# All projections of a two-layer decoder trunk with tokens stationary, results and residual stream turned in 32x32 blocks through DRAM

## The chip, the core and the metric

The kernel runs on one core of a Trainium2 chip. A core has a matrix engine (TensorE, PE in the profile; its weight loads are PEld), a vector engine (VectorE, DVE), a scalar engine (ScalarE, ACT), GpSimd (POOL) and SyncE (SP), each with its own in-order queue of instructions. DMA transfers are issued from SP's and ACT's queues here and carried out by 16 DMA engines. Working memory is SBUF (128 partitions); TensorE writes into PSUM, in banks of 128 x 512 float32. The metric is the time of one execution on the device in microseconds (us): the median of several runs.

## What is computed

256 tokens of width 2048 go through two layers. The first mixes tokens with gated linear attention (GLA, 4 heads, in chunks of 64 tokens), the second with forgetting attention (FoX, 12 heads, causal softmax with a decay). Each layer also attends with 4 heads to 256 memory tokens, and each has a gated MLP with a causal convolution of width 3. Cut to its steps:

```python
mem_n = rmsnorm(mem, norm_mem)
# layer 0
mk, mv = memory_kv(mem_n, mem_w_kv[0])
h = rmsnorm(x, norm_mix[0])
q, k, v, glr, og, mq = split_cols(h @ gla_w_in, ...)
o = rms(gla_chunked(q, k, v, g(glr))) * gn_gain * silu(og)
x = x + concat([o, memory_attention(mq, mk, mv)]) @ gla_w_out
x = x + conv_ffn(rmsnorm(x, norm_ffn[0]), ...)
# layer 1
k, v, fl = split_cols(rmsnorm(x, fox_kv_norm) @ fox_w_kv, ...)
q, mq = split_cols(rmsnorm(x, norm_mix[1]) @ fox_w_in, ...)
x = x + concat([fox_attention(q, k, v, cumsum(log_f)), memory_attention(mq, ...)]) @ fox_w_out
x = x + conv_ffn(rmsnorm(x, norm_ffn[1]), ...)
return rmsnorm(x, norm_final)

def conv_ffn(h, w_up, conv_w, conv_b, w_down):
    a, val = split_cols(causal_dwconv(h @ w_up, conv_w, conv_b), ...)
    return (jax.nn.silu(a) * val) @ w_down
```

All is float32. Weights are read once: some 430 MB.

## The kernel before, in words

**Precision.** Every large product is made of three: an operand is split into a high part that TensorE takes as it is (type fp32r) and a low part, the rest. The product is high x high + high x low + low x high. Activations stand in 16 tiles `A0..A15` (`bufA`) or `B0..B15` (`bufB`), one for each 128 features, with high and low halves of 256 tokens each (`split`, lines 332 to 340).

**Units and panels.** Weights come in units of 512 KB (1024 columns in each of 128 partitions). For each unit SP issues one load into `raw` (line 215), ACT makes the high part `whi` (line 218) and DVE the low part `wlo` (line 227), with four buffers for `raw` and three each for `whi` and `wlo`. These three are issued with a higher priority than what stands around them. A panel is a set of units that fills one set of accumulators; `_panels` lists them in the order in which they run.

**Two forms of a panel.** `proj_fm` (line 231, feature-major) has 256 outputs: a unit holds four chunks of 128 inputs, the weights are TensorE's stationary operand, and the high and low tokens side by side (512 columns) stream past `whi` (line 246), the high tokens alone (256 columns) past `wlo` (line 254). Its result lies with features in partitions; the two halves of the accumulator are added by an ACT copy and a DVE addition (`whole`, lines 263 and 265). It serves the keys of both attentions and of the memory, all queries and the output gate `og`: 34 panels of 4 units. `proj_tm` (line 282, token-major) has up to 512 outputs: a unit holds two chunks of inputs, the tokens are stationary, and the weights stream (lines 276, 277 and 280, 512 columns each, for both blocks of 128 tokens). Its result lies with tokens in partitions. It serves values, output projections and both MLP matrices.

**Turning in the MLP.** The MLP needs features in partitions for its convolution. `panel` (line 870) scales the result on ACT (line 876), transposes its 32x32 blocks on DVE (line 877), writes the 512 KB to DRAM (line 880) and reads it back in four transfers (line 885), which puts the blocks in their places. `later` (line 185) sets when this happens: so many units after the panel, counted by `passed` at each unit, and each step is queued behind that unit's cast on ACT:

```python
later((3, write), (6, read), (8, lambda: taken(j, base, u, 0)), (9, lambda: taken(j, base, u, 1)))
```

**The residual stream** `x` lies with tokens in partitions, four tiles of 512 features. After an output projection (`add_out`) has added a block to x, `preparing` (line 898) turns it on TensorE in 128x128 transposes (line 915), and `split` (line 340) makes the next stage's activations of it with the norm's gain; the norm's scale itself is applied to results (`nx.col` in token-major panels; `nx.row`, a broadcast made on TensorE at line 396, in feature-major ones; `nx.mixed` in the MLP).

**Ends of stages.** `proj_two` (line 300) runs two panels together: the first units of both, then the last `late` units of both, so that chunks that become ready late are asked for late. It is used for the MLP's second matrix with `late` 1. The output projections (`wo`) run one panel after the other and begin with the memory heads' chunks.

**Order around the change.** Memory keys and values of both layers; GLA: `gv` of head 0, memory queries, then for each head `gq`, `gk`, `gv` and the chunked core (`core`, line 600, fed by `gates`, line 580), two `og` panels before the last head's values and four after; `wo`; MLP; `fk`, `fv`, memory queries, `fq` with `attend` (line 785) at once for each head; `wo`; MLP; final norm.

Of the kernel before, what the change touches and what calls it, by code (L numbers as in the profile page):

```python
# [19 lines left out]
P = 128  # L20
# [22 lines left out]
OG_EARLY = 2  # L43
# [13 lines left out]
def _panels():  # L57
# [16 lines left out]

    for l in range(2):
        for j in range(2):
            fm(("mk", l, j), ("mem_w_kv", l), j * 256)
        tm(("mv", l), ("mem_w_kv", l), 512, 512)
    tm(("gv", 0), ("gla_w_in", 0), G_V, DV, more=[(G_R, RANK)])
    for j in range(2):  # L80
        fm(("mq", 0, j), ("gla_w_in", 0), G_MQ + j * 256)
    for h in range(GLA_H):
        fm(("gq", h), ("gla_w_in", 0), G_Q + h * DK)
        fm(("gk", h), ("gla_w_in", 0), G_K + h * DK)
        for j in range(OG_EARLY if h == GLA_H - 1 else 0):
            fm(("og", j), ("gla_w_in", 0), G_OG + j * 256)
        if h:
            tm(("gv", h), ("gla_w_in", 0), G_V + h * DV, DV)
    for j in range(OG_EARLY, 6):
        fm(("og", j), ("gla_w_in", 0), G_OG + j * 256)  # L90
    late = list(range(12, 16)) + list(range(12))

    def ffn(l):
        for p, (lo, hi) in enumerate(PARTS):
            for j in range(lo, hi, 2):
                turned(("up", l, j), ("ffn_w_up", l), [c + k * P for c in (0, HID) for k in (j, j + 1)])
            for f in range(4):
                tm(("down", l, p, f), ("ffn_w_down", l), f * 512, 512, list(range(lo, hi)))

    for f in range(4):  # L100
        tm(("wo", 0, f), ("gla_w_out", 0), f * 512, 512, late)
    ffn(0)
    for j in range(6):
        fm(("fk", j), ("fox_w_kv", None), F_K + j * 256)
# [3 lines left out]
    for j in range(2):  # L108
        fm(("mq", 1, j), ("fox_w_in", 0), FOX_H * HD + j * 256)
    for j in range(6):  # L110
        fm(("fq", j), ("fox_w_in", 0), j * 256)
    for f in range(4):
        tm(("wo", 1, f), ("fox_w_out", 0), f * 512, 512, late)
# [26 lines left out]
M_ID, M_ONE, M_FOX, M_SCAN, M_LVL = 0, 128, 256, 512, 768  # L140
M_PICK = M_LVL + NVER * len(LEVELS)
M_N = M_PICK + 2 * T
# [3 lines left out]
def _trunk(ctx: ExitStack, tc: tile.TileContext, xt, xtok, memt, wp, wgu, gns, gfin, cnv, par, msk, out):  # L146
# [6 lines left out]
    sm = ctx.enter_context(tc.tile_pool(name="small", bufs=2))  # L153
    pacc = ctx.enter_context(tc.tile_pool(name="pacc", bufs=4, space=PSUM))
# [7 lines left out]
    foxmask = mask[:, M_FOX : M_FOX + T]  # L162
# [41 lines left out]
    def load_unit(unit, pieces=1, before=None, pool=wpool, whole=False):  # L204
# [5 lines left out]
        for i in range(pieces):  # L210
            if before is not None:
                before(i)
            s = slice(i * w // pieces, (i + 1) * w // pieces)
            if not whole:
                loads.append(nc.sync.dma_start(raw[:, s], src[:, s]))
            elif i == 0:
                loads.append(nc.sync.dma_start(raw[:, :w], src))
            casts.append(S.activation(hi[:, s], raw[:, s], AF.Copy))  # L218
        return raw, hi, w

    def split_unit(unit, pieces=1, before=None, pool=wpool, whole=False):
        with tc.high_priority(offset=AHEAD):
            raw, hi, w = load_unit(unit, pieces, before, pool, whole)
# [6 lines left out]

    def proj_fm(key, src, evac, before=None):

        units = where[key]
        acc = [pacc.tile([P, 512], F32, name="acc", tag="acc") for _ in range(2)]
        base = min(min(u[1]) for u in units)
        for n, unit in enumerate(units):
            if before is None:
                hi, lo = split_unit(unit)
            else:
                hi, lo = split_unit(unit, 2, lambda half: before(n, half), whole=n > 0)  # L240
            todo = [(j, kc, c) for j, kc in enumerate(unit[1]) for c in range(2)]
            end = n == len(units) - 1

            def high(j, kc, c, stop=False):
                s = slice(j * 256 + c * P, j * 256 + (c + 1) * P)
                TE.matmul(acc[c], hi[:, s], src[kc - base], start=n == 0 and j == 0, stop=stop)  # L246

            kept = todo[-2:] if end else []
            for t in todo:
                if t not in kept:  # L250
                    high(*t)
            for j, kc, c in todo:
                s = slice(j * 256 + c * P, j * 256 + (c + 1) * P)
                TE.matmul(acc[c][:, :T], lo[:, s], src[kc - base][:, 0, :], start=False, stop=False)  # L254
            for t in kept:
                high(*t, stop=True)
        for c in range(2):
            evac(c, acc[c])

    def whole(a):  # L260

        t = sm.tile([P, T], F32, name="part1", tag="part1")
        S.activation(t, a[:, T:], AF.Copy)
        r = sm.tile([P, T], F32, name="wholes", tag="wholes")
        V.tensor_tensor(r, a[:, :T], t, ALU.add)
        return r
# [15 lines left out]
    def proj_tm(key, src, evac, spare=None):  # L282
# [7 lines left out]
        for i in range(len(units) + ahead):  # L290
            if i < len(units):
                ready[i] = split_unit(units[i], pool=wpool if spare is None or i < 3 else spare)
# [39 lines left out]
    def split(dst, i, src, g=None):  # L332

        hi, lo = dst[i][:, 0, :], dst[i][:, 1, :]
        if g is None:
# [6 lines left out]
    class Norm:  # L342


        def __init__(self, n, tag="x"):
            self.n, self.tag = n, tag
            self.acc = self.y = self.r = self.m = None

        def add(self, src):
            sq = sm.tile([P, T], F32, name="sq", tag="sq", bufs=2)  # L350
            S.activation(sq, src, AF.Square)
            if self.acc is None:
                self.acc = sq
            else:
                acc = sm.tile([P, T], F32, name="ssq", tag="ssq", bufs=2)
                V.tensor_tensor(acc, self.acc, sq, ALU.add)
                self.acc = acc
# [30 lines left out]
        def row(self):  # L388

            if self.r is None:  # L390
                y = self.col()
                dg = sm.tile([P, T], F32, name="dg", tag="sq", bufs=2)
                for b in range(2):
# [4 lines left out]
                                 bufs=2 if self.tag == "x" else 1)  # L398
# [42 lines left out]
    def mem_attention(pool, l, q, hd, dst):  # L441
# [11 lines left out]
        pts = pool.tile([P, 512], F32, name="pts", tag="ed", bufs=2)  # L453
# [14 lines left out]
    with tc.tile_pool(name="load", bufs=1) as lp:  # L468
# [3 lines left out]
        def take_mem(g, half):  # L472

            if g == 0:
# [4 lines left out]
                chunks = range(2 * half, 2 * half + 2)  # L479
            else:  # L480
                if half == 0:
                    nc.sync.dma_start(mraw[g][:, KC:], memt[g, :, KC:])
                    if g == 1:
                        nc.sync.dma_start(gains, gns)
                chunks = range(2 * half, 2 * half + 2)
            for i in chunks:
# [3 lines left out]
        def mk_out(l, j):  # L490
            def evac(c, a):
                o = mk[l][:, 2 * j + c, :]
                if l == 0:
                    S.activation(o, a[:, T:], AF.Copy)
                    V.tensor_tensor(o, o, a[:, :T], ALU.add)
                    if c == 1 and j == 1:
                        for f in range(MEM_H):
                            V.tensor_tensor(mk[0][:, f, :], mk[0][:, f, :], nrm.row(), ALU.mult)
                else:
                    V.tensor_tensor(o, whole(a), nrm.row(), ALU.mult)  # L500

            return evac
# [4 lines left out]
        def first_out(c, a):  # L507
            mk_out(0, 0)(c, a)
            if c == 1:
                nc.sync.dma_start(mask[:, :M_FOX], msk[:, :M_FOX])  # L510
                sq, acc = [lp.tile([P, 4, T], F32, name=n) for n in ("sq4", "ssq4")]
                with tc.issue_after(casts[-1].ins):
                    for g in range(4):
                        S.activation(sq if g else acc, mt[g], AF.Square)
                        if g:
                            V.tensor_tensor(acc, acc, sq, ALU.add)
                V.tensor_tensor(acc[:, :2, :], acc[:, :2, :], acc[:, 2:, :], ALU.add)
                V.tensor_tensor(acc[:, 0, :], acc[:, 0, :], acc[:, 1, :], ALU.add)
                nrm.acc = acc[:, 0, :]

        proj_fm(("mk", 0, 0), bufA, first_out, before=take_mem)
        proj_fm(("mk", 0, 1), bufA, mk_out(0, 1))
        xf = [lp.tile([P, T], F32, name=f"xf{i}") for i in range(KC)]
        with tc.issue_after(loads[-1].ins):
# [3 lines left out]
            nc.sync.dma_start(mask[:, M_FOX:], msk[:, M_FOX:M_PICK])  # L528
# [3 lines left out]
        for j in range(2):  # L532
            proj_fm(("mk", 1, j), bufA, mk_out(1, j))
            if j == 0:
                with tc.issue_after(loads[-1].ins):
                    for f in range(4):
                        nc.sync.dma_start(x[f], xtok[f])
                for f in range(4):
                    for b in range(2):
                        nx.add(f, b)  # L540
# [3 lines left out]
    def gla(nx):  # L544
# [507 lines left out]
```

## Time and profile before

| | |
|---|---|
| median of 3 runs | 2272.16 us (2272.04 to 2272.42) |
| profiled execution: its time, its span | 2272.27 us, 2270.5 us |
| granted TensorE clock in it | 0.998 |
| instructions | 30386, of them 10984 matmuls |
| HBM read, written | 449.46 MB, 25.18 MB |
| weight loads of 512 KB, issue to landing | 743, 4.1 us |

The span runs from the first to the last instruction that the profile shows. Rows of groups give line, engine, operation, output and inputs, shape and count, then busy time in us and mean ns of one, then idle time before them and what ended it. Rows of a timeline give start, length, engine, line, operation and count; matmuls overlap, so the time of one is read from the distance of two starts. A window's row gives its bounds, then for each engine busy time and number of instructions, the granted clock, the DMA engines' busy share and GB/s.

### The profile page before, as it was taken

How to read it: one execution, taken by the hardware profiler on the slowest of the kernel's cores; microseconds unless marked ns; L12 is line 12 of the kernel's file. 1: busy time of each engine (PE TensorE's matmuls, PEld its weight loads, DVE VectorE, ACT ScalarE, POOL GpSimd, SP SyncE). 2: the span in 40 equal slices, each digit the busy share in tenths (PEclk: the TensorE clock that was granted, in tenths of full speed). 3: DMA queues.
4: the chain of work that ended last, by engine and by line, in shares of the span. 5: the costliest groups of instructions: out<-in, count | busy, mean ns of one | idle time of the engine just before them, and what ended most of it. 6: DMA issues, size and time to landing. Idle time of an engine off the chain costs nothing.

```text
span 2270.5 us, 30386 instructions
## 1 busy us (share of the span) xinstructions
PE 2258.8 (99%) x10984; PEld 1914.9 (84%) x10984; DVE 1511.6 (67%) x2383; ACT 1239.7 (55%) x1873; POOL 2.9 (0%) x17
## 2 busy tenths in 40 slices
PE   9999999999999999999999999999999999999998
PEld 8889898888888888888888998888888888888886
DVE  7569987557665576646766557656676566755766
ACT  7555565546553465445665455555555355544654
POOL 0000000000000000000000000000000000000000
PEclk9999999999999999999999999999999999999999
DMA  8544455557775777657755564466877577766774
GB/s 323 196 161 161 156 170 179 191 195 237 250 231 192 231 237 243 214 195 244 238 197 184 177 199 161 159 204 196 257 241 224 193 228 248 240 204 208 237 248 150
DMA packets 224286, 476.65 MB, mean 210 GB/s; under 512 B 107772, under 2 KB 112264, under 8 KB 224008
## 3 DMA queue, kind: packets, MB, share of 16 engines
q1 hardware_dynamic: 124440, 427.77, 56.5%
q10 hardware_dynamic: 99696, 46.95, 7.6%
q8 instruction: 86, 1.41, 0.3%
q14 instruction: 64, 0.52, 0.1%
HBM read 449.46 MB, written 25.18 MB: 209 GB/s over the span
## 4 chain that ended last, share of the span: by engine, by line
PE 99%; DMA 0%; DVE 0%; ACT 0%; issue 0%; DVEq 0%
PE acc L276 26%; PE acc L277 26%; PE acc L280 26%; PE acc L246 11%; PE acc L254 6%; PE ps_s L915 0%; PE ps_s L669 0%; PE ps_t L439 0%; PE ps_s L446 0%; PE ps_o L457 0%; PE ps_s L794 0%; PE ps_o L810 0%; PE ps_o L688 0%; PE ps_s L588 0%; PE ps_t L396 0%; DMA raw<-wp 0%
## 5 line engine op out<-in xcount | busy, mean ns | idle before, releaser
L227 DVE TENSOR_TENSOR wlo<-raw,whi 128x1024 fp32r<-128x1024 f32 (+4 forms) x812 | 971.7, 1199 | 635.4 <-ACT whi L218 620.2
L218 ACT ACTIVATE whi<-raw 128x1024 fp32r<-128x1024 f32 (+4 forms) x812 | 842.7, 1039 | 871.4 <-PE acc L277 677.0
L277 PE MATMUL acc<-whi,B 128*128 128x512 f32 (+3 forms) x1440 | 547.6, 381 | 0.0
L276 PE MATMUL acc<-whi,B 128*128 128x512 f32 (+3 forms) x1440 | 547.5, 381 | 0.0
L276 PE MATMUL acc<-whi,A 128*128 128x512 f32 x1248 | 486.1, 390 | 0.0
L277 PE MATMUL acc<-whi,A 128*128 128x512 f32 x1248 | 485.5, 389 | 0.0
L280 PE MATMUL acc<-wlo,B 128*128 128x512 f32 (+3 forms) x1440 | 376.3, 381 | 0.0
L280 PE MATMUL acc<-wlo,A 128*128 128x512 f32 x1248 | 336.8, 390 | 0.0
L277 PEld LDWEIGHTS acc<-whi,B 128*128 128x128 f32 x1440 | 270.3, 188 | 46.5
L276 PEld LDWEIGHTS acc<-whi,B 128*128 128x128 f32 x1440 | 270.2, 188 | 46.3
L280 PEld LDWEIGHTS acc<-wlo,B 128*128 128x128 f32 x1440 | 267.7, 188 | 46.3
L277 PEld LDWEIGHTS acc<-whi,A 128*128 128x128 f32 x1248 | 234.3, 188 | 48.8
L276 PEld LDWEIGHTS acc<-whi,A 128*128 128x128 f32 x1248 | 234.2, 188 | 48.7
L280 PEld LDWEIGHTS acc<-wlo,A 128*128 128x128 f32 x1248 | 233.7, 188 | 48.0
L246 PE MATMUL acc<-B,whi 128*128 128x512 f32 x704 | 185.0, 398 | 0.0
L246 PEld LDWEIGHTS acc<-B,whi 128*128 128x128 f32 x704 | 125.5, 189 | 21.9
L246 PE MATMUL acc<-A,whi 128*128 128x512 f32 x384 | 103.5, 404 | 1.2 <-DVE A L340 1.2
L254 PEld LDWEIGHTS acc<-B,wlo 128*128 128x128 f32 x704 | 96.6, 190 | 7.2
L862 ACT ACTIVATE cv<-u,cw 128x256 f32<-128x256 f32 x176 | 96.0, 587 | 10.2 <-DMA u<-turned 10.2
L254 PE MATMUL acc<-B,wlo 128*128 128x256 f32 x704 | 101.1, 284 | 0.0
L863 DVE SCALAR_TENSOR_TENSOR cv<-u,cw,cv 128x256 f32<-128x256 f32 x176 | 77.8, 480 | 5.3 <-ACT cv L862 5.2
L246 PEld LDWEIGHTS acc<-A,whi 128*128 128x128 f32 x384 | 69.7, 192 | 13.5 <-DVE A L340 1.9
(200 smaller groups left out, 1234.3 us busy)
## 6 DMA issues: line engine op xcount, KB each, us to landing
raw<-wp SPq DMA_DIRECT2D x743, 512.0 KB, 4.1
turned<-square ACTq DMA_DIRECT2D x44, 512.0 KB, 4.3
u<-turned ACTq DMA_DIRECT2D x176, 128.0 KB, 5.0
raw<-wp SPq DMA_DIRECT2D x32, 384.0 KB, 3.1
raw<-wp SPq DMA_DIRECT2D x24, 388.0 KB, 3.6
raw<-wp SPq DMA_DIRECT2D x8, 400.0 KB, 3.1
xf<-xt SPq DMA_DIRECT2D x16, 128.0 KB, 4.3
x<-xtok SPq DMA_DIRECT2D x4, 512.0 KB, 7.3
```

Of the source, the lines that this page charges most:

```text
L218: casts.append(S.activation(hi[:, s], raw[:, s], AF.Copy))
L227: V.tensor_tensor(lo[:, s], raw[:, s], hi[:, s].bitcast(F32), ALU.subtract)
L246: TE.matmul(acc[c], hi[:, s], src[kc - base], start=n == 0 and j == 0, stop=stop)
L254: TE.matmul(acc[c][:, :T], lo[:, s], src[kc - base][:, 0, :], start=False, stop=False)
L276: TE.matmul(acc[:, :n], xh, hi[:, s], start=first and j == 0, stop=False)
L277: TE.matmul(acc[:, :n], xl, hi[:, s], start=False, stop=False)
L280: TE.matmul(a, xh, ls, start=False, stop=stop)
L862: S.activation(r, v[:, 2:], AF.Identity, bias=w[3], scale=w[2])
L863: V.scalar_tensor_tensor(r, v[:, 1 : T + 1], w[1], r, ALU.mult, ALU.add)
```

## The change

All panels take the token-stationary form. `proj_fm` and `whole` go; `mk`, `gq` with `gk`, `og`, `mq`, `fk` and `fq` become panels of 512 outputs whose columns are dealt so that a 32x32 transpose of blocks and a pass through DRAM bring features into partitions. `Turn` does for them what the MLP's `panel` did, and `to_features` scales, transposes, and sets write, read and use. The reads move runs of 32 tokens (128 bytes); the MLP's own turn keeps its runs of 64.

x is kept in the dealt order too, and `preparing` turns it with DVE and DRAM in place of TensorE. The turned x of the first MLP's end stays in DRAM and is read a second time for the queries' norm. GLA's output is split into the mixer's tiles without its gate, and the gate is applied when `og` has come, to the sum of both halves. Order: for each head `gv`, then `gq` and `gk` in one panel, with gates and core 7 and 9 units after it; `og` x 3; the memory queries last, with the attention at 8 to 11 units, inside the output projection. `attend` likewise runs 8 to 11 units after its panel. Pairs: the first two of `wo`, of `fk` and of the first MLP part's up panels run in `proj_two` with `late` 2 (the MLP's second matrix as before with 1); layer 0's `wo` reads its chunks in their plain order. Some buffers shrink: `u` 3 to 2, `bc` 2 to 1, `onorm` 9 to 3, the row of the norm 2 to 1. The final output is put back in order by the host.

```diff
-    def fm(key, w, c0, kcs=full, second=None):
-        cols = [(c0, 256)] if second is None else [(c0, 128), (second, 128)]
-        out.append((key, w, kcs, cols, 4))
+    def four(key, w, c0, kcs=full):
+        turned(key, w, [c0 + k * P for k in range(4)], kcs)
...
     for h in range(GLA_H):
-        fm(("gq", h), ("gla_w_in", 0), G_Q + h * DK)
-        fm(("gk", h), ("gla_w_in", 0), G_K + h * DK)
...
+        tm(("gv", h), ("gla_w_in", 0), G_V + h * DV, DV, more=[] if h else [(G_R, RANK)])
+        turned(("qk", h), ("gla_w_in", 0), [g + h * DK + k * P for g in (G_Q, G_K) for k in range(2)])
...
-    def proj_fm(key, src, evac, before=None):
...
+    class Turn:
+        def __init__(self, tag="turned", bufs=4):
+            self.square = tp.tile([P, 2, 16, 32], F32, name="square", tag="square", bufs=2)
+            self.rows = dp.tile([2, 4, 32, 4, 4, 32], F32, name=tag, tag=tag, bufs=bufs)
+        def put(self, b, src):
+            V.transpose(self.square[:, b], src.rearrange("p (c t) -> p c t", t=32))
+        def write(self):
+            nc.scalar.dma_start(self.rows.rearrange("b q i r k t -> (q i) b (r k t)"),
+                                self.square.rearrange("p b c t -> p b (c t)"))
+        def read(self, dst, blocks=range(4)):
+            for k in blocks:
+                nc.scalar.dma_start(dst(k).rearrange("p (n t) -> p n t", t=32),
+                                    self.rows[:, :, :, :, k, :].rearrange("b q i r t -> (i r) (b q) t"))
+    def to_features(scales, dst, *steps):
...
+            e = tp.tile([P, 512], F32, name="scaled", tag="scaled", bufs=2)
...
+                    S.activation(o, i, AF.Copy, scale=s()[:, b : b + 1])
+            held[0].put(b, e)
...
+                later((3, held[0].write), (6, read), *[(n, lambda step=step: step(got[0])) for n, step in steps])
...
+                proj_tm(("qk", hd), h, to_features(
+                    [(0, 2, lambda: nx.times(DK ** -0.5)), (2, 4, nx.col)], qk,
+                    (7, lambda t, hd=hd, bc=bc: bc.append(gates(hd))),
+                    (9, lambda t, hd=hd, v=v, bc=bc: core(hd, t[:, :2, :], t[:, 2:, :], v, bc[0]))))
             for j in range(3):
                 take_og(j)
...
+            proj_tm(("mq", 0), h, to_features(
+                [(0, 4, lambda: nx.times(-(HD ** -0.5)))], back,
+                *[(8 + c, lambda q, c=c: mem_attention(gp, 0, q[:, c, :], c, mix)) for c in range(4)]))
+            add_out(("wo", 0), mix, then, late=2)
...
+            proj_two([("fk", j) for j in range(2)], hk, [keys(j) for j in range(2)], 2)
+            def queries(f):
...
+                later((1 + 6 * f, read), (4 + 6 * f, lambda: halves(0)), (5 + 6 * f, lambda: halves(2)))
...
+            for j in range(3):
+                proj_tm(("fq", j), hq, to_features(minus, back, *[
+                    (8 + c, lambda q, c=c, j=j: attend(4 * j + c, q[:, c, :])) for c in range(4)]))
+            add_out(("wo", 1), mix, then, late=2)
...
-            for i in range(4 * f, 4 * f + 4, 2):
-                ps = work("s", 2)
...
-                        TE.transpose(o, x[f][:, c, k : k + P], ident)
...
+            turns[f].put(b, x[f][:, b, :])
...
+            later((3, turns[f].write), (6, read), (8, lambda: halves(0)), (9, lambda: halves(2)))
```

More of the change, by code (lines that the diff above doesn't have):

```diff
@@ L229, in split_unit @@
         return hi, lo
-    def proj_fm(key, src, evac, before=None):
[L233 to L266, printed above, removed]
     def products(accs, src, base, unit, hi, lo, first, last):
@@ L478, in take_mem @@
                     S.preload_act_table_set("natural_log_exp_and_others")
[L479 to L486, printed above, removed]
+            elif half == 0:
+                nc.sync.dma_start(mraw[g][:, KC:], memt[g, :, KC:])
+                if g == 1:
+                    nc.sync.dma_start(gains, gns)
@@ L487, in take_mem, with first @@
+            for i in range(2 * half, 2 * half + 2):
                 k = 4 * g + i
                 split(bufA, k, mt[g][:, i, :], mraw[0][:, k : k + 1])
[L490 to L502, printed above, removed]
+        def first(u, unit):
+            return split_unit(unit, 1 if u else 2, lambda piece: None if piece else take_mem(u // 2, u % 2))
@@ L504, in mv_out, with keys, scaled, dst @@
+        def keys(l):
+            def scaled(got):
+                for f in range(MEM_H):
+                    V.tensor_tensor(mk[0][:, f, :], mk[0][:, f, :], nrm.row(), ALU.mult)
+            def dst():
+                return lambda k: mk[l][:, k, :]
+            return to_features([(0, 4, nrm.col if l else None)], dst, *([] if l else [(9, scaled)]))
         def mv_out(l):
             return lambda b, a: S.activation(mv[l][:, b, :], a, AF.Copy, scale=nrm.col()[:, b : b + 1])
[L507 to L519, printed above, removed]
@@ L521, in _trunk @@
-        proj_fm(("mk", 0, 0), bufA, first_out, before=take_mem)
-        proj_fm(("mk", 0, 1), bufA, mk_out(0, 1))
+        proj_tm(("mk", 0), bufA, keys(0), before=first)
+        nc.sync.dma_start(mask[:, :M_SCAN], msk[:, :M_SCAN])
+        sq, acc = [x[f].rearrange("p b (c t) -> p (b c) t", t=T) for f in range(2)]
+        with tc.issue_after(casts[-1].ins):
+            for g in range(4):
+                S.activation(sq if g else acc, mt[g], AF.Square)
+                if g:
+                    V.tensor_tensor(acc, acc, sq, ALU.add)
@@ L742, in fox @@
+            for f in range(4):
+                queries(f)
+            proj_tm(("fk", 2), hk, keys(2))
             cs = fp.tile([P, T], F32, name="fc")
@@ L921, in preparing @@
[L921 to L938 removed]
+            got = []
```

362 lines of the change are left out of this document (180 added, 182 removed).

## The prediction

> **What bounds the kernel now.** I read the page's shares first, then its chain of work that ended last, then windows, to see whether the bound is the same in every stage.
>
> ```profile
> span 2270.5 us, 30386 instructions
> PE 2258.8 (99%) x10984; PEld 1914.9 (84%) x10984; DVE 1511.6 (67%) x2383; ACT 1239.7 (55%) x1873; POOL 2.9 (0%) x17
> PE 99%; DMA 0%; DVE 0%; ACT 0%; issue 0%; DVEq 0%
> ```
>
> TensorE is busy for the whole span and the chain is TensorE by itself. A busy PE could still hide slow stretches, so here are a GLA stretch, the first forgetting-attention panels, the query panels, an FFN up stretch and a down stretch.
>
> ```profile
> 200.00:300.00 100.00, 100.00 (x679) 90.65 (x678) 93.86 (x227) 60.60 (x107) 0.00 (x0) 1.00 0.49 159
> 1205.00:1272.00 67.00, 67.00 (x386) 59.78 (x385) 41.10 (x66) 30.14 (x42) 0.00 (x0) 1.00 0.53 173
> 1362.00:1442.00 80.00, 80.00 (x471) 71.03 (x471) 60.15 (x161) 45.97 (x102) 0.00 (x0) 1.00 0.48 156
> 550.00:600.00 50.00, 50.00 (x222) 41.42 (x221) 33.99 (x47) 29.09 (x41) 0.00 (x0) 1.00 0.79 250
> 2000.00:2050.00 50.00, 50.00 (x223) 41.39 (x222) 26.76 (x26) 19.69 (x20) 0.00 (x0) 1.00 0.59 195
> ```
>
> Columns are the stretch, its length, then busy time of PE, weight loads, DVE, ACT and POOL, granted clock, DMA share and GB/s. PE is full everywhere at clock 1.00. The one engine near it is DVE in the GLA stretch (93.86 of 100). So a microsecond of PE work that goes is a microsecond of span, as long as nothing new makes PE wait, and an edit on another engine is worth nothing unless it does that.
>
> **The panels.** A unit is 512 KB of weights (1024 columns in each partition). The feature-major form spends 8 matmuls of 512 columns and 8 of 256 on it, the token-stationary form 12 of 512: the same 6144 streamed columns, in 16 instructions or 12. Both run undisturbed in the first 40 us:
>
> ```profile
> 22.48 2.00 PE L246 MATMUL acc<-A,whi 128*128 128x512 f32 x8
> 24.32 1.11 PE L254 MATMUL acc<-A,wlo 128*128 128x256 f32 x8
> 25.28 2.00 PE L246 MATMUL acc<-A,whi 128*128 128x512 f32 x8
> 27.12 1.12 PE L254 MATMUL acc<-A,wlo 128*128 128x256 f32 x8
> 28.07 1.55 PE L246 MATMUL acc<-A,whi 128*128 128x512 f32 x6
> ...
> 33.61 0.39 PE L276 MATMUL acc<-whi,A 128*128 128x512 f32 x1
> ...
> 36.33 0.39 PE L276 MATMUL acc<-whi,A 128*128 128x512 f32 x1
> ```
>
> From 22.48 to 28.07 are two feature-major units, 2.795 us each; from 33.61 to 36.33 is one token-stationary unit, 2.72 us. The saving is 0.075 us a unit. The number of units comes from the groups:
>
> ```profile
> L246 PE MATMUL acc<-B,whi 128*128 128x512 f32 x704 | 185.0, 398 | 0.0
> L246 PE MATMUL acc<-A,whi 128*128 128x512 f32 x384 | 103.5, 404 | 1.2 <-DVE A L340 1.2
> ```
>
> 704 + 384 = 1088 matmuls, 8 a unit, are 136 units. All of them change form: 136 x 0.075 = **10.2 us** off PE. The token-stationary slot is 2.72 / 12 = 227 ns, so the 256-column slot is (2.795 - 8 x 0.227) / 8 = 122 ns, more than half of 227; that is the whole gain. The Trainium skill (TensorE: Matmul & The Clock Gate, Back-to-back issue gap) has an isolated warm gap of N / 2.4 + 2.5 ns. By it four matmuls fewer would save 10 ns a unit and 1.4 us in all (an estimate from that page); the rows, 75 ns a unit, do not agree, and I go by them.
>
> **The transposes of the residual.** `preparing` turns x on PE, 8 transposes for each of 4 column blocks, for three norms:
>
> ```profile
> L915 PE MATMUL ps_s<-mask,x x96: 270/272/273, 411.6 to 1547.3; 128*128 128x128 f32 x96
> ...
> 456.72 0.39 PE L280 MATMUL acc<-wlo,A 128*128 128x512 f32 x1
> 456.95 0.38 PE L915 MATMUL ps_s<-mask,x 128*128 128x128 f32 x2
> 457.08 0.48 PE L280 MATMUL acc<-wlo,A 128*128 128x512 f32 x1
> 457.40 0.82 PE L915 MATMUL ps_s<-mask,x 128*128 128x128 f32 x6
> 457.97 0.71 PE L280 MATMUL acc<-wlo,A 128*128 128x512 f32 x2
> 458.52 0.40 PE L276 MATMUL acc<-whi,A 128*128 128x512 f32 x1
> ```
>
> 456.72 to 458.52 is 1.80 us, and holds four L280 matmuls (4 x 0.227 = 0.91). The eight transposes cost 0.89 us; 96 / 8 = 12 such sets are **10.7 us**, and all go. Two broadcast rows go as well: the first layer's `nx` and the shared key/value norm now use only the column. One is here:
>
> ```profile
> 53.13 1.52 PE L246 MATMUL acc<-A,whi 128*128 128x512 f32 x6
> 54.49 0.59 PE L396 MATMUL ps_t<-dg,mask 128*128 128x256 f32 x2
> 54.74 0.81 PE L246 MATMUL acc<-A,whi 128*128 128x512 f32 x2
> 55.39 1.11 PE L254 MATMUL acc<-A,wlo 128*128 128x256 f32 x8
> ```
>
> Eight L246 took 2.26 us with it and 1.84 us without (22.48 to 24.32): 0.42 us, twice **0.8 us**. The attentions and the GLA core keep their small matmuls.
>
> **What comes in on DVE and ACT.**
>
> ```profile
> L265 DVE TENSOR_TENSOR wholes<-acc,part 128x256 f32<-128x256 f32 x64 | 26.9, 421 | 31.2 <-ACT part L263 30.9
> L877 DVE STREAM_TRANSPOSE square<-scaled 128x512 f32<-128x512 f32 x88 | 57.5, 690 | 0.8 <-ACT scaled L876 0.8
> L263 ACT ACTIVATE part<-acc 128x256 f32<-128x256 f32 x64 | 24.2, 379 | 53.8 <-PE acc L246 53.7
> L876 ACT ACTIVATE scaled<-acc,mixed 128x512 f32<-128x512 f32 x88 | 55.2, 675 | 1.9 <-DVE mixed L410 1.9
> ```
>
> The 34 old panels become 17 of 512 outputs, so 34 scaled copies and 34 transposes; x adds 3 x 4 x 2 = 24 transposes. DVE gains 58 x 0.690 = 40 us, and 24 instructions of 256 columns (the core's split, the gate's add) at 0.42 = 10 us; it loses 64 adds at 0.421 and as many products with the row, 54 us. ACT gains 34 x 0.675 = 23 us and loses 64 x 0.379 = 24 us. In one GLA head DVE loses 4 x 0.84 = 3.4 us and gains 2 x 0.69 + 3 x 0.42 = 2.6, so its 94% stays where it is. All this lies beside PE: nothing. Without that cover GLA would be DVE's, and the saving of its 64 units of this kind (64 x 0.075 = 4.8 us) would not show.
>
> **What comes in on the queues.** 29 turns (17 panels, 12 of x) of one write and four reads, and four more sets of reads of the kept turns, are 161 issues on ACT's queue. The FFN already turns this way:
>
> ```profile
> q10 hardware_dynamic: 99696, 46.95, 7.6%
> turned<-square ACTq DMA_DIRECT2D x44, 512.0 KB, 4.3
> u<-turned ACTq DMA_DIRECT2D x176, 128.0 KB, 5.0
> L885 ACTq DMA_DIRECT2D u<-turned x176: 366/529/1531, 507.9 to 2205.3; - x176
> DMA u<-turned: 10.2, 13
> DMA to landing us min/median/max: 3.0/5.0/6.5
> ```
>
> An issue takes 0.53 us, so 161 x 0.53 = 85 us of ACT over the kernel, which has 45% free. The write is issued three units after the panel, the read six, the first use eight: 2 x 2.72 = 5.4 us for a landing of 5.0. That is why ACT waited 13 times, 10.2 us, for `u` in 44 panels. In the FFN a cast stands behind that wait and three cast buffers hide it. Behind ACT's waits for the write (for DVE's transpose) and the read (for the write to land) the casts stand as before. But in five panels (queries of both layers) the first user is now a PE matmul, and behind that stands everything on PE.
>
> The stage ends have to cover this latency. x's last block is turned 9 units after it is added, and a pair with `late=2` first asks for it after 2 x 6 = 12 units: covered. The attentions of the last query panel are issued at units 8 to 11 of the output pair, and their chunks are asked for from unit 13. One head takes this long now:
>
> ```profile
> 1436.25 0.38 PE L793 MATMUL ps_s<-fkt,fq 128*128 128x128 f32 x2
> ...
> 1449.25 0.42 DVE L337 TENSOR_TENSOR B<-ps_o,B 128x256 fp32r<-128x256 f32 x1
> ```
>
> That is 13.4 us from scores to split, with PE's own work between. With three cast buffers a cast, and what is issued after it, runs about two units ahead, so the last head starts about unit 9 and has 4 to 5 units, 11 to 14 us. It may just miss, in both output stages. I bound all new waits by 0 and by 12 us: five first uses at 10.2 / 13 = 0.8 us are 4, and the two ends at up to 4 us each are 8. A start a little earlier (less is asked of the first loads, the memory being spread over 8 units instead of 4) may give back up to 1.5. I take 1.5 us lost, nearer to the low end, because the FFN runs the same pipeline with PE full.
>
> **The sum.** 10.2 + 10.7 + 0.8 - 1.5 = 20.2 us. The profiled execution took 2272.27 us for its span of 2270.5; the median of the runs is 2272.16, the same to 0.1. 2272.2 - 20.2 = **2252 us**.
>
> **Rivals.** *New waits at the ends.* The query reads and the two output stages, and ACT held in GLA where DVE is late with its transposes, cost 12 us or somewhat more: 2272.2 - 21.7 + 12 = 2262.5, between 2257 and 2268. For it: 13.4 us against 11 to 14. Against: the FFN shows no PE wait.
>
> *The panels give nothing.* If a 256-column matmul were no dearer by the column and the 0.075 us came from something else in that stretch, only 10.7 + 0.8 would stay: 2272.2 - 11.5 + 1.5 = 2262. Against: the undisturbed rows, both from one clock and one stretch of 40 us. The gap of the Trainium skill (TensorE: Matmul & The Clock Gate, Back-to-back issue gap) points to this case.
>
> *Slower: the turn's small pieces fill the DMA engines.* Its place is every new panel. The new reads move 128-byte runs, 4096 a panel, 256 for each of the 16 engines; the FFN's run is 256 bytes, 128 for each engine. The up stretch has a DMA share of 0.79, the down stretch 0.59: 0.20 x 21.8 us (8 units) = 4.4 us a panel, so at most 34 ns a packet. Without turns the panels sit at 0.53, which leaves 0.47 x 21.8 = 10.2 us a panel. At 34 ns 256 packets take 8.7 us and still fit beside a write of about 1 us; from about 36 ns on the weights come late. At 40 ns the excess is 1.0 us in each of some 33 sets, 33 us: 2284. Against: a run of half the length should not take longer. The Trainium skill (DMA: Bandwidth & Descriptors, Specifications) wants 512 bytes or more, below which the engine does a read-modify-write; no run here shows a 128-byte run yet.
>
> *No gain:* waits of 20 us spread over the stages, about 2270.
>
> **How the numbers follow.** Forecast (2248 to 2257) 0.68; new waits 0.13; panels without gain 0.05; DMA bound 0.08; no gain 0.04; better than 2248, 0.02. A measurement tells about 0.2% (4.5 us) from no change, so faster is below 2267.7 and slower above 2276.7: faster 0.68 + 0.13 + 0.05 + 0.02 less 0.01 = 0.87, same 0.05, slower 0.08. The range takes the forecast, the waits and the panels: 2247 to 2267.
>
> **What would show it.** Right: no feature-major lines, 96 transposes gone, 12-matmul units of 2.72 us in the key and query panels, PE full in each window, span about 2250. Wrong: PE waiting for `back` or for the mixers' splits at the start of the output stages, fk windows with a DMA share near 1, casts waiting on DMA, or packets of the turned reads above 36 ns.

## The result and the profile after

| | before | after |
|---|---|---|
| median of 12 runs each, us | 2271.96 (2270.9 to 2272.42) | 2271.99 (2267.08 to 2278.49) |
| profiled execution, us | 2272.27 | 2272.12 |
| its span, us | 2270.5 | 2270.3 |

The ratio is 1.0001, interval 0.9992 to 1.001: the time is the same, 20 us above the forecast of 2252 and outside its range. A forecast of "no change" would have been right about the time and wrong about the kernel, for much has moved. The page of after (span, shares, chain of waits, ACT's DMA queue):

```profile
span 2270.3 us, 29243 instructions
PE 2246.3 (99%) x10340; PEld 1875.3 (83%) x10340; DVE 1499.7 (66%) x2329; ACT 1239.8 (55%) x1852; POOL 2.9 (0%) x15
q10 hardware_dynamic: 244864, 79.46, 14.3%
PE 89%; ACTq 3%; DMA 3%; DVE 2%; issue 1%; ACT 1%; SPq 0%; DVEq 0%
```

PE is 12.5 us less busy than before (2258.8) in the same span. The shares still say 99%; the chain says what is wrong: PE held 99% of it before, now 89%, and ACTq is new, the part of ScalarE's queue that issues DMAs. A window of before, then windows of after:

```profile
1150.00:1200.00 50.00, 50.00 (x238) 41.62 (x237) 36.62 (x53) 37.09 (x79) 0.31 (x1) 1.00 0.53 179
...
400.00:450.00 50.00, 49.06 (x221) 39.85 (x220) 29.04 (x46) 26.38 (x54) 0.14 (x2) 1.00 0.63 190
550.00:600.00 50.00, 50.00 (x222) 41.42 (x221) 34.47 (x50) 30.11 (x42) 0.00 (x0) 1.00 0.81 255
1150.00:1200.00 50.00, 46.77 (x199) 37.90 (x198) 29.04 (x39) 25.39 (x51) 0.31 (x1) 0.97 0.75 219
1250.00:1300.00 50.00, 47.72 (x251) 44.02 (x251) 28.57 (x41) 30.09 (x48) 0.00 (x0) 1.00 0.96 235
1500.00:1550.00 50.00, 46.47 (x203) 37.51 (x202) 31.49 (x48) 25.31 (x46) 0.00 (x0) 1.00 0.83 240
2000.00:2050.00 50.00, 50.00 (x222) 41.44 (x221) 27.08 (x26) 19.30 (x19) 0.00 (x0) 1.00 0.61 197
```

Inside the FFN (550, 2000) PE is full as before. It waits mainly around the ends of the stages, where turns of the residual stream and of panels stand close together. Worked out from the trace, each stage cut at its first panel matmul; "work" is its matmuls by number and undisturbed slot (227 ns for 512 columns, 122 for a feature-major panel's 256, 216 and 108 for the small matmuls of 256 and 128), "rest" is what the stage took beyond that. The GLA core's 288 matmuls of 64 and 96 columns have no slot in this count; before as after they stand in GLA's rest, which is therefore not waiting alone:

| stage | work before / after | rest before | rest after | rest, reads on SP (e2_sp) |
|---|---|---|---|---|
| memory | 89.1 / 87.9 | 2.2 | 2.3 | 2.6 |
| GLA | 270.6 / 256.9 | 16.2 | 19.9 | 19.3 |
| first output | 90.1 / 96.1 | 0.3 | 4.1 | 1.1 |
| first FFN | 722.1 / 718.6 | 0.2 | 5.9 | 0.3 |
| FoX keys, values | 135.2 / 132.2 | 1.2 | 4.6 | 1.6 |
| queries | 112.6 / 103.5 | 0.2 | 0.4 | 0.4 |
| second output | 94.5 / 98.7 | 0.6 | 5.2 | 0.8 |
| second FFN | 719.5 / 718.6 | 0.0 | 0.1 | 0.0 |
| sum | 2233.7 / 2212.6 | 20.9 | 42.5 | 26.1 |

PE's work fell by 21.1 us, where the terms of the forecast gave 21.7. The rest grew by about as much. (Memory attention moved from GLA to the first output stage.)

What PE waits for (us in total, times, longest): the only two rows of before, then two of after. Then ACT's timeline of after ahead of the longest wait, at 1178, and PE's at it:

```profile
PE ps_o L181 <- DVE B L178: 1.4, 1, 1.4
PE acc L246 <- DVE A L340: 1.2, 1, 1.2
...
PE acc L228 <- ACT whi L207: 10.0, 10, 2.3
...
PE ps_s L461 <- DMA back<-turned: 0.8, 1, 0.8
```

```profile
1164.18 1.06 ACT L207 ACTIVATE whi<-raw 128x1024 fp32r<-128x1024 f32 x1 [0.30 <-PE acc L229]
1164.19 6.87 ACTq L301 DMA_DIRECT2D back<-xturned  x4
1171.10 1.06 ACT L207 ACTIVATE whi<-raw 128x1024 fp32r<-128x1024 f32 x1 [5.86 <-DMA back<-xturned]
1171.18 5.82 ACTq L301 DMA_DIRECT2D back<-xturned  x4
1177.11 1.06 ACT L207 ACTIVATE whi<-raw 128x1024 fp32r<-128x1024 f32 x1 [4.94 <-issue]
```

```profile
1178.22 0.79 PE L228 MATMUL acc<-whi,A 128*128 128x512 f32 x1 [2.29 <-ACT whi L207]
1178.81 0.63 PE L229 MATMUL acc<-whi,A 128*128 128x512 f32 x1
1179.24 0.63 PE L228 MATMUL acc<-whi,A 128*128 128x512 f32 x1
```

PE waits for `whi`, the cast of the weights. The casts are late because ACT's queue is in order and stands still: one set of four reads (line 301, `Turn.read`) takes 6.87 us only to issue, a second one behind a single cast takes 5.82. Between 1164.2 and 1177.1 ACT makes two casts where PE used up more than four units. After the wait of 2.29 us TensorE also runs at half rate: its matmuls start 0.43 us apart (1178.81 to 1179.24) until about 1181.4, in place of 0.227, and the granted clock of 1178.1 to 1181.4 is 0.50. The Trainium skill (TensorE: Matmul & The Clock Gate, HAM oscillation) warns of PE gaps above about 3.4 us; here 2.29 us was enough.

The durations of these issues in after (min/median/max), and the rows of the whole line:

```profile
L301 ACTq DMA_DIRECT2D back<-xturned x64: 366/630/4731, 433.1 to 1556.4; - x64
L301 ACTq DMA_DIRECT2D back<-turned x32: 366/607/2932, 306.4 to 1450.2; - x32
...
  ACT whi L207: 18.8, 5
...
DMA to landing us min/median/max: 3.0/5.1/9.1
```

The median looks harmless. By place in a set of four the medians are 0.37, 0.61, **2.02** and 0.62 us; a set holds ACT's queue for 4.6 us in the median and 9.4 at most, and line 301 takes 152.9 us for 132 issues, 1.16 each. The FFN's sets, which the forecast priced this from, have 0.37, 0.53, 0.53 and 0.53.

### The profile page after: what moved, and what is told of

It reads as the page before. It is cut to its first block, busy times and chain, and to the rows that moved or that the text cites. A ratio compares the mean times of both kernels' runs of the same rounds, so it can differ in the third digit from the quotient of the medians.

```text
span 2270.3 us, 29243 instructions
## 1 busy us (share of the span) xinstructions
PE 2246.3 (99%) x10340; PEld 1875.3 (83%) x10340; DVE 1499.7 (66%) x2329; ACT 1239.8 (55%) x1852; POOL 2.9 (0%) x15
## 3 DMA queue, kind: packets, MB, share of 16 engines
q10 hardware_dynamic: 244864, 79.46, 14.3%
## 4 chain that ended last, share of the span: by engine, by line
PE 89%; ACTq 3%; DMA 3%; DVE 2%; issue 1%; ACT 1%; SPq 0%; DVEq 0%
PE acc L228 29%; PE acc L232 29%; PE acc L229 29%; ACTq L301 3%; DMA xturned<-square 1%; ACT whi L207 1%; DVE wlo L216 1%; DMA turned<-square 1%; PE ps_s L659 0%; DVE B L347 0%; DVE square L293 0%; PE ps_t L454 0%; PE ps_s L461 0%; PE ps_o L472 0%; DMA mt<-memt 0%
## 5 line engine op out<-in xcount | busy, mean ns | idle before, releaser
L228 PE MATMUL acc<-whi,B 128*128 128x512 f32 (+3 forms) x1792 | 687.3, 384 | 6.8 <-ACT whi L207 6.8
L229 PE MATMUL acc<-whi,B 128*128 128x512 f32 (+3 forms) x1792 | 684.4, 383 | 0.0
L228 PE MATMUL acc<-whi,A 128*128 128x512 f32 x1440 | 563.9, 393 | 4.1 <-ACT whi L207 3.2
L229 PE MATMUL acc<-whi,A 128*128 128x512 f32 x1440 | 561.0, 391 | 0.0
L232 PE MATMUL acc<-wlo,B 128*128 128x512 f32 (+3 forms) x1792 | 469.7, 383 | 0.0
L228 PEld LDWEIGHTS acc<-whi,B 128*128 128x128 f32 x1792 | 336.4, 188 | 70.4 <-ACT whi L207 10.0
L232 PE MATMUL acc<-wlo,A 128*128 128x512 f32 x1440 | 387.1, 390 | 0.3 <-DVE wlo L216 0.3
L229 PEld LDWEIGHTS acc<-whi,B 128*128 128x128 f32 x1792 | 336.0, 188 | 59.2
L232 PEld LDWEIGHTS acc<-wlo,B 128*128 128x128 f32 x1792 | 333.4, 188 | 60.5
L228 PEld LDWEIGHTS acc<-whi,A 128*128 128x128 f32 x1440 | 271.1, 188 | 64.3 <-ACT whi L207 6.7
L229 PEld LDWEIGHTS acc<-whi,A 128*128 128x128 f32 x1440 | 271.2, 188 | 55.8 <-DVE A L347 0.2
L859 DVE SCALAR_TENSOR_TENSOR cv<-u,cw,cv 128x256 f32<-128x256 f32 x176 | 77.7, 479 | 6.4 <-ACT cv L858 6.3
L860 DVE SCALAR_TENSOR_TENSOR cv<-u,cw,cv 128x256 f32<-128x256 f32 x176 | 77.0, 478 | 0.0
L877 DVE STREAM_TRANSPOSE square<-scaled 128x512 f32<-128x512 f32 x88 | 57.6, 690 | 0.8 <-ACT scaled L876 0.8
L876 ACT ACTIVATE scaled<-acc,mixed 128x512 f32<-128x512 f32 x88 | 55.1, 675 | 1.9 <-DVE mixed L425 1.9
```

The source lines that it names most:

```text
L228: TE.matmul(acc[:, :n], xh, hi[:, s], start=first and j == 0, stop=False)
L229: TE.matmul(acc[:, :n], xl, hi[:, s], start=False, stop=False)
L232: TE.matmul(a, xh, ls, start=False, stop=stop)
L859: V.scalar_tensor_tensor(r, v[:, 1 : T + 1], w[1], r, ALU.mult, ALU.add)
L860: V.scalar_tensor_tensor(r, v[:, :T], w[0], r, ALU.mult, ALU.add)
L876: S.activation(e, a, AF.Copy, scale=nx.mixed(picks)[:, b : b + 1])
```

## The experiments

All times are medians in us; each ratio is to the kernel before on the same chip.

**e1_spread: the reads one unit apart.**

```diff
-later((3, held[0].write), (6, read), *[(n, ...) for n, step in steps])
+later((3, held[0].write), *[(5 + k, lambda k=k: read(k)) for k in range(4)], *[(n, ...) for n, step in steps])
```

with the same at the two places where x is read, and the uses one or two units later.

> The changed kernel, with the four reads of each turn one unit apart (units 5, 6, 7, 8 after the panel) in place of all at unit 6; the uses of the late chunks move back by one or two units. Queue theory: four reads of 1024 runs issued together fill the queue and hold ACT 3 to 9 us, the casts stand behind them and PE runs out of weights. Then each issue falls under 0.7 us, PE's waits of some 19 us at the stage ends go, and the time is about 2253 us (2249 to 2258). Latency theory (the turned data lands too late for the stage ends): the last chunk now lands later still, so no gain, 2272 to 2280. Bandwidth theory (the DMA engines are the bound): the same bytes and packets, 2272 unchanged.

2257.16 (2254.92 to 2259.61), ratio 0.9935 [0.992, 0.995]. ACT's timeline in it, where the reads do come apart:

```profile
1225.48 0.37 ACTq L301 DMA_DIRECT2D back<-xturned  x1
...
1228.20 0.37 ACTq L301 DMA_DIRECT2D back<-xturned  x1
...
1230.98 0.37 ACTq L301 DMA_DIRECT2D back<-xturned  x1
```

Same reads, same bytes, other spacing. They come apart only in part: of the 132 reads 52 are issued 1.5 us or more after the issue before them, with a median of 0.37 us (two took over 1 us), and 60 within 0.2 us of it, with a median of 0.61 and up to 3.95. All 132 together take 119.4 us in place of 152.9. So it is mostly the issue that follows closely on others that is long.

**e1_spread_x: only x's reads apart.**

> The same spreading for the turns of the residual stream alone (and the second reading for the queries); the turned panels' reads stay together. Queue theory: of the 19 us of PE waits, those where two sets of x follow each other (around 440, 465, 487, 1170, 1195, 1254, 1510 and 1530 us, 15 us together) go, the panels' (around 360 and 385 us, 2.5 us) stay: about 2257 us. Latency and bandwidth theories: 2272 or more.

2265.66 (2260.87 to 2268.0), ratio 0.997 [0.9958, 0.9981], a miss by some 9 us. The first FFN loses its waits and the keys lose most of theirs, but the first output stage has a rest of 7.8 us, with this row among PE's waits:

```profile
PE ps_s L461 <- DMA back<-turned: 3.2, 1, 3.2
```

So x's sets are only a part. That the attentions' sets, left in one piece, cost the rest is the likely reading; no run spreads them alone.

**e2_sp and e2_pool: the reads issued by another engine.**

```diff
-                nc.scalar.dma_start(dst(k).rearrange("p (n t) -> p n t", t=32),
+                nc.sync.dma_start(dst(k).rearrange("p (n t) -> p n t", t=32),
```

and `nc.gpsimd` in the other.

> The changed kernel with the reads of the turns issued from SP's queue in place of ACT's. Queue theory: ACT is free, and now the weight loads stand behind the reads; four raw buffers are 10.9 us, a load takes 4.2, so a hold of up to 6 us is hidden: 2252 to 2262 us. Latency and bandwidth theories: unchanged, 2272.

> The changed kernel with the reads of the turns issued from POOL's queue, which has nothing else to do. Queue theory: nothing stands behind the reads, about 2252 us, unless an issue from POOL takes so long that the turned data comes late; then PE waits for it at the stage ends and in the query panels, 2260 to 2300. Latency and bandwidth theories: 2272 or more.

From SyncE 2255.53 (2254.58 to 2256.03), ratio 0.9927 [0.9912, 0.9942]; from GpSimd 2255.33 (2254.45 to 2261.98), 0.9925 [0.9909, 0.9942]. The page, PE's wait for the casts, two windows and SP's timeline with SyncE:

```profile
span 2253.6 us, 29217 instructions
PE 2241.0 (99%) x10340; PEld 1875.5 (83%) x10340; DVE 1503.3 (67%) x2329; ACT 1244.8 (55%) x1852; POOL 2.9 (0%) x15
```

```profile
PE acc L228 <- ACT whi L207: 0.5, 1, 0.5
...
1150.00:1200.00 50.00, 50.00 (x222) 41.42 (x221) 38.89 (x63) 30.72 (x63) 0.00 (x0) 1.00 0.90 256
1200.00:1250.00 50.00, 50.00 (x222) 41.41 (x221) 28.19 (x32) 24.64 (x31) 0.00 (x0) 1.00 0.97 261
```

```profile
1159.95 4.24 SPq L301 DMA_DIRECT2D back<-xturned  x4
1164.29 2.28 SPq L206 DMA_DIRECT2D raw<-wp  x2
1166.66 1.00 SPq L301 DMA_DIRECT2D back<-xturned  x2
1167.76 3.20 SPq L206 DMA_DIRECT2D raw<-wp  x1
```

The set still takes 4.24 us to issue, and the weights' loads (`raw`) stand behind it. The casts now wait 62.4 us in all for their loads (30.9 in after), but `raw` has four buffers and those loads were issued early, so PE hardly notices: its wait for casts falls from 10.0 to 0.5 us, and the stage table's last column to 26.1. That is the separating run: the transfers and bytes are those of after, only the queue that is held is another, and 16.5 us return. With GpSimd:

```profile
L301 POOL DMA_DIRECT2D back<-xturned x64: 882/882/893, 438.9 to 1545.1; - x64
```

An issue is 0.88 us there almost without exception (at most 1.02). The profiled execution is the slowest of the four, 2261.98; in it PE waited 4.8 us once for the memory attention's reads (`PE ps_s L461 <- DMA back<-turned: 4.8, 1, 4.8`), so turned data that comes late can cost something too.

**e3_pe_turn: x for both MLP norms turned on TensorE as before** (transposes come back at those two places, the rest of the change stays; the rows of the up matrix are ordered to match).

> The changed kernel with the turn of x for the two MLP norms undone: TensorE transposes it as before (8 sets of 8 transposes at 0.89 us, 7.1 us of PE work back), with the columns in the dealt order and the first MLP matrix's rows ordered to match. The key/value norm still goes through DRAM. Queue theory: the waits at the ends of both output stages (3.4 us around 420 to 490 us, 4.3 us around 1506 to 1535 us) go, so 2272 - 7.7 + 7.1 = 2271 us; each turn of x through ACT's queue costs about what it saves. If those waits came from the attention at the stage ends instead, they stay: 2279.

2279.94 (2275.83 to 2282.71), ratio 1.0035 [1.0021, 1.0048], 9 us above the expectation and at the 2279 of its rival, that the waits come from the attentions. The stages do not bear out either alone. The second output stage lost its waits as the queue theory has it (rest 1.0 in place of 5.2); in the first output stage the rest is 7.9 in place of 4.1, and elsewhere too waits grew:

```profile
PE acc L228 <- ACT whi L207: 9.1, 8, 2.5
PE ps_s L461 <- DMA back<-turned: 2.3, 1, 2.3
```

One of these, 2.5 us, stands in the memory stage, which the edit does not touch: the reads of `mk` held ACT for 7.87 us there in this run. The same set holds the queue for different times in different runs (4.84 us in after), which may be why the times of after scatter by 11 us and those of e2_sp by 1.5; but e2_pool's scatter by 7.5, so this is not shown.

**e4_eight: eight reads of 512 runs for each set of four.**

```diff
+                for b in range(2):
+                    nc.scalar.dma_start(dst(k)[:, b * P : (b + 1) * P].rearrange("p (n t) -> p n t", t=32),
+                                        self.rows[b, :, :, :, k, :].rearrange("q i r t -> (i r) q t"))
```

> The changed kernel with each read of a turn cut in two by token block: eight issues of 512 runs in place of four of 1024; the same runs and bytes. By runs: the first four issues of a set are short (0.4 to 0.7 us) and the long ones come from the fifth on; by transfers: from the third on, as before. ACT is held as long as before and a little longer: 2272 to 2282 us either way.

2278.45 in a single execution. By place the medians are 0.37, 0.53, 0.53, 0.55, **0.89**, 0.46, 0.52, 0.52. The first four, 2048 runs together, behave as the FFN's four; the first long one is the fifth, as the third was with 1024 runs a read. So in the medians it is not the number of transfers that fills the queue, it is the number of runs, at about 2048; single sets differ. The set as a whole holds ACT longer, 6.6 us in the median.

**e5_runs64: x turned in runs of 64 tokens,** 256 bytes, half as many.

```diff
+        def put64(self, b, src):
+            sq = self.square.rearrange("p b c t -> p (b c t)").rearrange("p (c b t) -> p c b t", c=16, b=2)
+            V.transpose(sq[:, :, b, :], src.rearrange("p (c t) -> p c t", t=32))
...
-            turns[f].put(b, x[f][:, b, :])
+            turns[f].put64(b, x[f][:, b, :])
```

with writes, reads and splits to match (two splits in place of one).

> The changed kernel, reads still four together on ACT's queue, but the residual stream's turns are laid out so that a read moves runs of 64 tokens (256 bytes): 512 runs a read and 2048 a set in place of 1024 and 4096, the same bytes. The splits behind them take two instructions each in place of one (128 more on ACT and DVE). If the queue holds by the number of runs (about 2048 before an issue must wait), the sets of x issue in about 2.1 us as the MLP's do, their 15 us of PE waits go, the panels' stay: about 2257 us (2254 to 2263). If it holds by transfers or by bytes: unchanged, 2272.

2262.86 (2262.15 to 2264.6), ratio 0.9964 [0.9951, 0.9977]. That is inside the expected range and 6 us above its centre. x's reads now have medians of 0.37, 0.53, 0.53, 0.56, close to the FFN's, with the same bytes, so runs and not bytes count. Yet some are still long, probably where they meet a queue that other sets have filled:

```profile
L307 ACTq DMA_DIRECT2D back<-xturned x64: 366/528/3929, 435.0 to 1542.5; - x64
```

**e6_sp_nopair: reads on SyncE, and the panels at the stage ends one after the other** in place of pairs. In this kernel the first panels' last chunks are multiplied before the turned values are written into them; that wait is left out, and its time says nothing of it.

> The kernel with reads on SP's queue, with the three kinds of pairs that ask late for four chunks undone: output projections, first keys and first up panels run one panel after the other. Then a first panel asks for its last chunks at units 5 to 7 while the turned block is split at units 8 and 9 after its own panel. If the pairs are what covers the way through DRAM, PE waits 2 to 4 units (5 to 11 us) at the start of the first MLP, the keys, and the second MLP, and less at the two output projections: 2255 + 15 to 45 = 2270 to 2300 us. If the cover isn't needed: 2255.

2256.9 (2255.89 to 2259.49), ratio 0.994 [0.9923, 0.9956]. Pairing by itself costs nothing that shows beside e2_sp. What the pairs cover stays untried.

**e7_read8: the reads two units later,** still on ACT.

```diff
-later((3, turns[f].write), (6, read), (8, lambda: halves(0)), (9, lambda: halves(2)))
+later((3, turns[f].write), (8, read), (10, lambda: halves(0)), (11, lambda: halves(2)))
```

and the same in `to_features`.

> The changed kernel with every set of reads issued two units of weights later (unit 8 in place of 6 after the block is done; what uses the turned blocks is moved two units later with it); the reads stay on ScalarE's queue, back to back. It tells two causes of ScalarE's stops apart. Theory one, the reads' issue itself holds the queue (sets of 4x1024 runs hold it 3 to 9 us, and two sets follow each other): the sets are as long as before, only later, the waits of TensorE stay about 21 us in all: 2264 to 2274 us. Theory two, a read stands on the queue until the write of the same block has landed in DRAM: two units (about 6 us) more would have let the write land, the stops shrink to about 2 us a set and TensorE's waits fall by some 14 us: 2254 to 2260 us.

2260.38 (2258.88 to 2262.25), ratio 0.9951 [0.9937, 0.9964]: just above the second theory's range and 4 us under the first's. Yet the issues of all turned reads, the FFN's included, took 249.1 us in all, 245.5 in after (on line 301 158.5 and 152.9): in sum nothing was shorter, so in the main they had not been waiting for the write. ACT in e7:

```profile
1166.57 1.06 ACT L207 ACTIVATE whi<-raw 128x1024 fp32r<-128x1024 f32 x1 [1.66 <-PE acc L229]
1166.58 5.44 ACTq L301 DMA_DIRECT2D back<-xturned  x4
1172.14 1.06 ACT L207 ACTIVATE whi<-raw 128x1024 fp32r<-128x1024 f32 x1 [4.51 <-PE acc L229]
1172.16 4.80 ACTq L301 DMA_DIRECT2D back<-xturned  x4
1177.07 1.06 ACT L207 ACTIVATE whi<-raw 128x1024 fp32r<-128x1024 f32 x1 [3.87 <-DMA back<-xturned]
```

Here too the first read goes 0.01 us after its cast, as in after. At this place the gain is a threshold. In after PE could have started at 1178.22 - 2.29 = 1175.93, 11.75 us after the cast at 1164.18. The same distance from 1166.57 is 1178.32; the third cast ended at 1177.07 + 1.06 = 1178.13. Two sets that held ACT for 10.4 us fitted, two that held it for 12.8 did not. Why these two were shorter is not settled; in after the second write was issued 0.5 us ahead of the first set, here 6 us, so less may have been in the queue. At the second output stage the first read of after was issued 1.1 us after the start of the cast ahead of it (1499.15 to 1500.27), so it may have waited that long for its write; a small part of the second theory can hold there. How the rest of e7's gain comes about is not shown.

**e8_sp_runs64: e2_sp and e5_runs64 together.**

> The reads issued from SyncE (as in e2_sp) and the residual stream turned in runs of 64 tokens, 256 bytes in place of 128 (as in e5_runs64); the other turns keep 128 bytes. Theory (ScalarE's queue is all that the issues cost): nothing waits for the issues on SyncE, so fewer runs give nothing more: 2253 to 2257 us, within 0.1% of e2_sp's 2255.5, less the extra splits' cost if any. Rival (the reads' traffic also disturbs the loads of the weights at the ends of the stages): halving x's packets gives a further 2 to 4 us, 2250 to 2253 us.

2256.73 (2255.51 to 2257.57), ratio 0.9934 [0.992, 0.9947]. With ACT's queue free, halving x's packets gives nothing more: whatever the traffic of the small runs does to the loads of the weights, it does not cost measurable time. e2_sp, and e2_pool and e1_spread within its interval, are some 0.7% under the kernel before.

## Why the prediction was wrong

**The step that failed** is the cost of the queues: "An issue takes 0.53 us, so 161 x 0.53 = 85 us of ACT over the kernel, which has 45% free." The 0.53 came from the FFN's reads, 512 runs each. The new ones have 1024, as the rival on small pieces counted itself ("4096 a panel"), and this was used for the DMA engines and not for the issue. The reads on line 301 took 1.16 us each. The second half of the step is the worse one: 45% free is an average over the kernel, and an issue cannot be spread over it. It stands on an in-order queue with the casts behind it, in sets of 4.6 us and, for two sets on end, of 8.5 to 13.9 us, against the lead that three cast buffers give (11.75 us at 1176). The forecast said itself that behind ACT's waits "the casts stand as before", and did not price the issue as such a wait.

**What was right.** The saving on PE: 10.2 + 10.7 + 0.8 = 21.7 us forecast, 21.1 by count. The count uses the forecast's own slots; what bears them out is that the query stage keeps a rest of 0.2 us with the old form and 0.4 with the new, and that the span falls by 16.9 with the reads off ACT's queue. DVE's and ACT's added work lay beside PE: DVE's sum went from 1511.6 to 1499.7, and in GLA (95.7 to 372.5 in after) DVE was busy for 215.75 of 276.8 us. That panels of the token-stationary form are cheaper by more than matmuls fewer times a fixed gap is shown by e2_sp: without a gain from the panels even waits of nothing would have given 2272.2 - 11.5 = 2260.7, and it took 2255.5. By the Trainium skill's isolated gap of N / 2.4 + 2.5 ns (TensorE: Matmul & The Clock Gate, Back-to-back issue gap), which that section says under-counts at small N, it could not have come under that by more than 1.4 us (an estimate from that page); the trace does not agree with the isolated gap.

**The new waits** were bounded by 12 us and are 21.6. The rival of new waits named the query reads and the attentions at the two output stages. With the reads on SyncE these cost little: the output stages keep 1.1 and 0.8 us of rest, so the "13.4 us against 11 to 14" was covered there; e2_pool's 4.8 us shows that it was close. Most of the loss (first FFN's end 5.7 us, keys and values 3.4, second output 4.6, part of the first output's 3.8) went with the reads off ACT's queue. The case that came true in its time, "no gain", waits of 20 us spread over the stages, had a chance of 0.04 and no mechanism.

**The slower rival** is refuted. ACT's queue took 14.3% of 16 engines' span, 7.6% before: 16 x (0.143 x 2270.3 - 0.076 x 2270.5) = 2433 us more. Were all of it the 33 sets of 4096 new runs, a 128-byte packet would take 18 ns; the rival needed 36. (The trace's packet records give a mean of 13.3 ns, 18.3 for 256 bytes and 195 for 4096.) The Trainium skill asks for 512 bytes or more for line rate (DMA: Bandwidth & Descriptors, Specifications). The trace agrees: 128 bytes in 13.3 ns are 9.6 GB/s on one engine, 4096 in 195 ns are 21. But that price was not what PE paid: with the reads on SyncE PE is full at a DMA share of 0.97 (1200 to 1250 in e2_sp).

**What stays open.** e2_sp is 3.5 us above the forecast: its rests are 5.2 us more than before, 3.1 of them in GLA. GLA's rest is above that of before in every variant, and the rows of waits do not name the cause. And what makes one set of reads take 4 us and the next, alike, 9 is seen only in part.

## What to carry to other kernels

Price a DMA issue as time of the in-order queue it stands on, by its runs and by its place in a burst, and ask what else that queue must do in time; here the casts, whose lead is three buffers. A median of the issues hides this: read the maximum and the place in the set. Put strided reads on a queue whose other work has slack (here SyncE or GpSimd), and look for waits at stage ends, where several bursts meet, since PE at 99% does not show them.

## What the hardware showed that I had not expected

- With about 2048 runs of a burst issued, the next DMA issue from ACT is the long one, whether these were two transfers of 1024 (median 2.02 us, at most 4.73 for any issue of after) or four of 512 (0.89), of 128 bytes each. On SP a set takes 4.2 us in the median too, with issues of up to 4.03. From GpSimd an issue is a nearly flat 0.88 us. The Trainium skill (DMA: Bandwidth & Descriptors, Issuing engines are not separate DMA queues) says that starting DMAs on several engines saves only the sequencer's time to initiate them, usually small beside the DMA; the runs agree that it is the sequencer's time, and here that time was worth 16.5 us.
- 2.29 us without a matmul were enough for TensorE to run at half rate for some 3 us after; after's windows show it as a clock of 0.97 (1150 to 1200). The length alone does not decide: in e4_eight a gap of 1.99 us, up to 1541.32, did the same, and in e3_pe_turn one of 2.41 us, up to 1207.96, left the matmuls 0.23 us apart.
